# One weight fetch moved ahead of another in a decoder trunk, and the last quarter of its last row tile summed in a bank of its own

## The chip, the cores and the metric

The kernel runs on one core of a Trainium2 chip. The metric is the device time of one execution in microseconds (us), as the median of three runs. The engines are called as the profile calls them: PE (TensorE, the matmuls) with PEld (its weight loads), DVE (VectorE), ACT (ScalarE), POOL (GpSimd), and SP, whose queue issues the DMAs.

## What is computed

Two layers; each is a token mixer and then a convolutional feed-forward net, each followed by a residual sum and a LayerNorm. All is float32, for 256 tokens of 1024 channels.

```python
def mixer_sublayer(x, ...):
    proj = x @ w_in
    x_rnn, g_rnn, q_lat, kv_lat, k_rope, gate_a, gate_b = jnp.split(proj, _split_points(), axis=-1)
    y_rnn = jax.nn.gelu(g_rnn) * rg_lru(causal_dwconv(x_rnn, conv_w, conv_b), ...)
    y_mla = mla_attention(q_lat, kv_lat, k_rope, cos, sin, q_norm_g, w_uq, kv_norm_g, w_ukv)
    merged = jax.nn.sigmoid(gate_a) * y_rnn + jax.nn.sigmoid(gate_b) * y_mla
    return merged @ w_out

def conv_ffn(x, w_up, ffn_conv_w, ffn_conv_b, w_down):
    h = causal_dwconv(x @ w_up, ffn_conv_w, ffn_conv_b)
    h_gate, h_val = jnp.split(h, 2, axis=-1)
    return (jax.nn.gelu(h_gate) * h_val) @ w_down

for l in range(DEPTH):                                   # DEPTH = 2
    x = layer_norm(ALPHA * x + mixer_sublayer(x, ...), ln1_g[l], ln1_b[l])
    x = layer_norm(ALPHA * x + conv_ffn(x, ...), ln2_g[l], ln2_b[l])
```

Attention has 16 heads, is causal, and takes its values (64 per head) from `kv_lat` through a part of `w_ukv`. `gate_b` is 1024 columns wide.

## The kernel before

**Split products.** A float32 product is made of three matmuls on rounded parts: `mm3` (L193) multiplies high by high (L194), high by low (L195) and low by high (L196). So each weight block that arrives by DMA is split: ACT copies it into the high part (L185), DVE subtracts that from the raw block into the low part (L186). `load_split` (L169) issues the DMA on SP's queue and then both halves of the split. Raw blocks rotate through 4 buffers, split halves through 6 buffers named `w`; some weights go to slots named `wsh` and `wsl` instead.

**What sets the order.** PE runs in the order in which the program is written; the other engines' instructions are put in order when the program is built, by a scheduler that works on estimates of its own, and each engine then runs its list strictly in that order. Within a layer the mixer's steps are written in the order of the string `ORDER` (L43). A step is a letter and its arguments. Those that matter here:

- `P` with a hexadecimal digit fetches and splits one block of the list `FETCH` (L41) ahead of its use. `Pe` is the last, `("gb", 3)`: the weights of pair 3 (counted from 0) of branch B's gates. `h3` (`sig_b`, L672) multiplies them: 48 matmuls into the tile `proj`, then a sigmoid on ACT into `sB`.
- `w0` (`value_begin`, L734) fetches and splits the first half of the values' weights, one block of 128x1024; `v00` and `v01` (L738) use it, into `vps`.
- `b0`, `q0`, `k0`, `p0` and so on: for a group of four heads, fetch its query and key weights, multiply queries (`qps`), keys (`kps`) and rotary parts (`peps`), and copy them out of PSUM, half by ACT and half by DVE (for keys L731 and L732, into `k96`). `R1` and `r0`, `r1` are the recurrence's scan (L664) and its product with the gate (L668).
- `s`, `f`, `y`: scores of a pair of heads (`sps`; DVE L764 to L775, ACT L768 and L770), their transposes (`ptp`, which ACT copies to `pT`, L790), and the values (`yps`, L802). DVE multiplies `yps` by the sigmoid and adds branch A (`mg`, L809 and L810), and ACT and DVE split the sum into `mhi` (L199) and `mlo` (L200).
- `o01` and `o00` are the output projection of chunk 0 for row tiles 1 and 0; each tile has two of the four PSUM accumulators `oacc`.

**PSUM.** Two sets of four banks rotate: `acc` hands out the ones for `kps`, `qps`, `vps`, `oacc` and `dacc`, `bank` the ones for `proj`, `sps`, `ptp` and `yps`. A bank is free again when all who read its last tile have read it.

**The end of a layer.** `finish` (L360) issues the last products of the down projection for row tile 0, then LayerNorm's `tile` (L392) for it, then those of row tile 1 and its `tile`. A tile takes two halves of 512 columns: for each, residual plus sum (L400) and statistics (L404); then L405 and L406 on DVE, the inverse root on POOL (L407), and for the last layer L411 and L414 and the store.

Of the kernel before, what the change touches and what calls it, by code (L numbers as in the profile page):

```python
# [11 lines left out]
F32 = mybir.dt.float32  # L12
# [3 lines left out]
ALU = mybir.AluOpType  # L16

P = 128
# [24 lines left out]
ORDER = (  # L43
# [5 lines left out]
)  # L49
HELD = 4  # L50
WARM = 8
LINE = 256
STEP = 32
# [72 lines left out]
def trunk(ctx, tc, x_tok, x_chan, pos, wts, par, lnrow, consts, out):  # L126
    nc = tc.nc
    A = nc.scalar
    V = nc.vector
# [2 lines left out]

    cpool = ctx.enter_context(tc.tile_pool(name="cpool", bufs=1))
    tiny = ctx.enter_context(tc.tile_pool(name="tiny", bufs=2))
    wpool = ctx.enter_context(tc.tile_pool(name="wpool", bufs=1))
    big = ctx.enter_context(tc.tile_pool(name="big", bufs=1))
    sm = ctx.enter_context(tc.tile_pool(name="sm", bufs=2))
# [5 lines left out]
    def bank(name):  # L143
        return pp.tile([P, 512], F32, tag="pb", name=name)
# [48 lines left out]
    def mm3(o, lh, ll, rh, rl, start, stop):  # L193
        T.matmul(o, lhsT=lh, rhs=rh, start=start, stop=False)  # L194
        T.matmul(o, lhsT=lh, rhs=rl, start=False, stop=False)  # L195
        T.matmul(o, lhsT=ll, rhs=rh, start=False, stop=stop)  # L196
# [10 lines left out]
    spare = bank("spare")  # L207
    for _ in range(WARM):
        T.matmul(spare[:, :P], lhsT=idle, rhs=idle, start=True, stop=True)
# [23 lines left out]
    for i in range(1, 4):  # L233
# [9 lines left out]
        out=mask[:, P:], in_=mask[:, P:], pattern=[[-1, P]],  # L243
# [108 lines left out]
    def out_last(accs, t, n, wts_of, act_of, hc):  # L352
        for h, c in hc:
            hi, lo = wts_of(c)
            ah, al = act_of(c)
            mm3(accs[t][h], ah[:, t * P:(t + 1) * P], al[:, t * P:(t + 1) * P],
                hi[:, 512 * h:512 * h + 512], lo[:, 512 * h:512 * h + 512],
                False, c == n - 1)

    def finish(ln, accs, n, wts_of, act_of, late):  # L360
        out_last(accs, 0, n, wts_of, act_of, [(h, n - 1) for h in range(2)])
        ln.tile(0, accs)
        hc = [(h, c) for h in range(2) for c in range(n - late, n)]
        out_last(accs, 1, n, wts_of, act_of, hc[:-HELD])
        if not ln.last:
            ln.turn(0)
        out_last(accs, 1, n, wts_of, act_of, hc[-HELD:])
        ln.tile(1, accs)

# [8 lines left out]
    class LayerNorm:  # L378
# [10 lines left out]
            if not last:  # L389
                self.xs = [(slot("xhi", F32R), slot("xlo", F32R)) for _ in range(2)]  # L390

        def tile(self, t, accs):  # L392
            l, last = self.l, self.last
            z = big.tile([P, D], F32, tag="xres", name="z", bufs=4, align_bytes=LINE)
            st = tiny.tile([P, 2, 6], F32, tag="st", name="st")
            mv = tiny.tile([P, 2], F32, tag="mv", name="mv")
            rs = tiny.tile([P, 1], F32, tag="rs", name="rs")
            hs = [slice(512 * h, 512 * h + 512) for h in range(2)]
            for h in range(2):
                V.scalar_tensor_tensor(  # L400
                    out=z[:, hs[h]], in0=self.xres[t][:, hs[h]], scalar=ALPHA, in1=accs[t][h],
                    op0=ALU.mult, op1=ALU.add,
                )
                V.bn_stats(st[:, h], z[:, hs[h]])  # L404
            V.bn_aggr(mv, st.rearrange("p a b -> p (a b)"))  # L405
            V.tensor_scalar(out=rs, in0=mv[:, 1:2], scalar1=EPS, scalar2=None, op0=ALU.add)  # L406
            G.tensor_tensor(out=rs, in0=rs, in1=nhalf[:, 0:1], op=ALU.pow)  # L407
            g, b = self.gb
            if last:
                for h in range(2):  # L410
                    V.scalar_tensor_tensor(out=z[:, hs[h]], in0=z[:, hs[h]], scalar=mv[:, 0:1],  # L411
                                           in1=g[:, hs[h]], op0=ALU.subtract, op1=ALU.mult)
                for h in range(2):
                    V.scalar_tensor_tensor(out=z[:, hs[h]], in0=z[:, hs[h]], scalar=rs,  # L414
                                           in1=b[:, hs[h]], op0=ALU.mult, op1=ALU.add)
                    nc.sync.dma_start(out=out[t * P:(t + 1) * P, hs[h]], in_=z[:, hs[h]])
                return
            nmr = tiny.tile([P, 1], F32, tag="nmr", name="nmr")
            V.scalar_tensor_tensor(out=nmr, in0=mv[:, 0:1], scalar=-1.0, in1=rs,
                                   op0=ALU.mult, op1=ALU.mult)  # L420
            for c in (0, 256):
                V.tensor_scalar(out=z[:, c:c + 256], in0=z[:, c:c + 256], scalar1=mv[:, 0:1],
                                scalar2=rs, op0=ALU.subtract, op1=ALU.mult)
            A.activation(z[:, hs[1]], z[:, hs[1]], AF.Identity, scale=rs, bias=nmr)
            self.res.append(z)
# [84 lines left out]
    ends = (None, None)  # L510
    for l in range(DEPTH):
# [337 lines left out]
        later[0] = False  # L849
        ln = LayerNorm(l, 0, xres, False)  # L850
        finish(ln, oacc, 8, lambda c: ow[c], mer_of, 5)
        tp = [bank("upt") for _ in range(NB)]

# [85 lines left out]
        for j in range(NPAIR - LAG, NPAIR - 1):  # L939
            out_chunk(dacc, j, dw[j], hq[j], (0, 1) if j < NPAIR - LATE else (0,))  # L940
        ln = LayerNorm(l, 1, xres, l == DEPTH - 1)
        finish(ln, dacc, NPAIR, lambda c: dw[c], lambda c: hq[c], LATE)
        if l < DEPTH - 1:
            xs, xres = ln.xs, ln.res
            lat = []
            lacc = [[bank("latp") for _ in range(2)] for _ in range(NT)]
            for i, kc in enumerate(KORD):
                if i == 5:
                    ln.turn(1)
                    ends = ln.ends  # L950
# [113 lines left out]
```

## Time and profile before

| what | us |
|---|---|
| median of 3 runs (785.43 to 787.75) | 785.65 |
| the profiled execution, device time | 786.62 |
| its span, from the first to the last instruction | 784.8 |
| PE busy | 770.5 |
| DVE busy | 646.0 |
| ACT busy | 510.2 |
| PE idle for another engine, all waits of 0.2 us and more together | 6.5 |

The profiled execution is 0.97 us above the median, and 1.82 us of it lie outside the span. TensorE's granted clock is 0.995 of full speed over the span. A timeline row gives the start, the time to the end of the last instruction merged into the row, engine, line, operation, output and inputs, shape, and the count; the square brackets give the idle time ahead of it and who ended that. DVE and ACT rows overlap a little, since an instruction starts before the one ahead has drained. PE's matmuls overlap by more than half, so for PE it is the distance of starts that counts.

### The profile page before, as it was taken

What the parts mean: (1) busy time and instruction counts of PE and PEld (TensorE: products, weight loads), DVE (VectorE), ACT (ScalarE), POOL (GpSimd) and SP (SyncE); (2) the same over time, 40 slices, a digit from 0 to 9 for tenths busy, and PEclk for the clock granted to TensorE, in tenths of its full rate; (3) what the DMA queues carried; (4) which work ended last, traced back from release to release, by engine and by line L of the source; (5) the groups of instructions that cost most, each with busy time, mean ns of one, the idle gap of its engine ahead of it and who ended that gap; (6) DMA issues with size and microseconds to landing.
All of it is one profiled execution on the core that took longest, in us unless ns stands there. A gap on an engine that the chain in (4) does not pass through costs nothing.

```text
span 784.8 us, 14452 instructions
## 1 busy us (share of the span) xinstructions
PE 770.5 (98%) x5712; PEld 723.9 (92%) x5712; DVE 646.0 (82%) x1260; ACT 510.2 (65%) x910; POOL 10.2 (1%) x27
## 2 busy tenths in 40 slices
PE   9999899999999999999999999999999999999996
PEld 9999899878999999999899999998799999999994
DVE  6998789997699977668777897999877998677665
ACT  6856887783677565556374579688657775565540
POOL 0000000000000000000000000000000000000000
PEclk9999999999999999999999999999999999999999
DMA  9855436525457555535715554463515675746311
GB/s 320 331 210 215 151 112 240 207 63 210 162 199 262 203 199 210 195 126 196 268 52 218 169 208 134 172 231 123 193 76 186 261 251 182 247 162 200 123 54 54
DMA packets 26467, 144.76 MB, mean 184 GB/s; under 512 B 3360, under 2 KB 7072, under 8 KB 11808
## 3 DMA queue, kind: packets, MB, share of 16 engines
q1 hardware_dynamic: 26400, 143.84, 51.7%
q8 instruction: 45, 0.74, 0.4%
q14 instruction: 22, 0.18, 0.1%
HBM read 140.68 MB, written 1.05 MB: 181 GB/s over the span
## 4 chain that ended last, share of the span: by engine, by line
PE 89%; DVE 4%; ACT 4%; issue 2%; DMA 1%; SPq 0%; DVEq 0%
PE proj L196 16%; PE proj L194 15%; PE proj L195 15%; PE dacc L194 6%; PE dacc L195 6%; PE dacc L196 6%; PE oacc L194 2%; PE oacc L196 2%; PE oacc L195 2%; PE sps L759 2%; DVE w L186 2%; PE yps L802 2%; PE ptp L787 1%; PE latp L195 1%; PE latp L196 1%
## 5 line engine op out<-in xcount | busy, mean ns | idle before, releaser
L196 PE MATMUL proj<-xhi,w 128*128 128x256 f32 x1216 | 338.0, 278 | 3.0 <-DVE w L186 3.0
L194 PE MATMUL proj<-xhi,w 128*128 128x256 f32 x1216 | 338.1, 278 | 0.0
L195 PE MATMUL proj<-xlo,w 128*128 128x256 f32 x1216 | 337.7, 278 | 0.0
L186 DVE TENSOR_TENSOR w<-raw,w 128x1024 fp32r<-128x1024 f32 (+5 forms) x226 | 241.8, 1087 | 52.4 <-ACT w L185 51.9
L185 ACT ACTIVATE w<-raw 128x1024 fp32r<-128x1024 f32 (+5 forms) x226 | 208.8, 952 | 86.6 <-PE proj L196 73.4
L196 PEld LDWEIGHTS proj<-xhi,w 128*128 128x128 f32 x1216 | 228.8, 188 | 3.4 <-DVE w L186 3.4
L195 PEld LDWEIGHTS proj<-xlo,w 128*128 128x128 f32 x1216 | 229.2, 189 | 1.3
L194 PEld LDWEIGHTS proj<-xhi,w 128*128 128x128 f32 x1216 | 228.9, 188 | 1.4
L905 DVE SCALAR_TENSOR_TENSOR u<-proj,par,u 128x255 f32<-128x255 f32 (+1 forms) x176 | 83.4, 478 | 25.4 <-ACT u L902 23.3
L902 ACT ACTIVATE u<-proj,par 128x256 f32<-128x256 f32 x88 | 49.7, 564 | 72.7 <-DVE u L905 47.8
L194 PE MATMUL dacc<-wsh,hh 128*128 128x512 f32 x192 | 75.2, 392 | 0.0
L195 PE MATMUL dacc<-wsl,hh 128*128 128x512 f32 x192 | 75.1, 391 | 0.0
L196 PE MATMUL dacc<-wsh,hl 128*128 128x512 f32 x192 | 74.7, 389 | 0.0
L186 DVE TENSOR_TENSOR wsl<-raw,wsh 128x1024 fp32r<-128x1024 f32 (+2 forms) x66 | 70.4, 1077 | 0.0
L185 ACT ACTIVATE wsh<-raw 128x1024 fp32r<-128x1024 f32 (+2 forms) x66 | 59.5, 938 | 0.0
L196 PEld LDWEIGHTS dacc<-wsh,hl 128*128 128x128 f32 x192 | 36.1, 188 | 7.8
L194 PEld LDWEIGHTS dacc<-wsh,hh 128*128 128x128 f32 x192 | 36.0, 188 | 6.4
L195 PEld LDWEIGHTS dacc<-wsl,hh 128*128 128x128 f32 x192 | 36.1, 188 | 6.0
L199 ACT ACTIVATE hh<-u 128x256 fp32r<-128x256 f32 x48 | 19.8, 411 | 24.7 <-DVE u L913 24.6
L194 PE MATMUL oacc<-w,mhi 128*128 128x512 f32 x64 | 26.7, 417 | 0.0
L196 PE MATMUL oacc<-w,mlo 128*128 128x512 f32 x64 | 25.3, 395 | 0.0
L195 PE MATMUL oacc<-w,mhi 128*128 128x512 f32 x64 | 25.2, 393 | 0.0
(213 smaller groups left out, 1130.2 us busy)
## 6 DMA issues: line engine op xcount, KB each, us to landing
raw<-in_wts SPq DMA_DIRECT2D x114, 1024.0 KB, 4.9
raw<-in_wts SPq DMA_DIRECT2D x8, 832.0 KB, 4.9
gb<-in_lnrow SPq DMA_DIRECT2D x8, 512.0 KB, 7.7
raw<-in_wts SPq DMA_DIRECT2D x4, 672.0 KB, 4.0
raw<-in_wts SPq DMA_DIRECT2D x7, 336.0 KB, 6.1
raw<-in_wts SPq DMA_DIRECT2D x4, 512.0 KB, 4.8
xres<-in_x_tok SPq DMA_DIRECT2D x2, 512.0 KB, 6.0
k<-krot SPq DMA_DIRECT2D x8, 128.0 KB, 2.4
```

Source lines behind the costliest of these rows:

```text
L185: behind(A.activation(h, w, AF.Copy), after[0])
L186: lo_ins = V.tensor_tensor(out=lo[:, c - a:d - a], in0=w, in1=h.bitcast(F32), op=ALU.subtract)
L194: T.matmul(o, lhsT=lh, rhs=rh, start=start, stop=False)
L195: T.matmul(o, lhsT=lh, rhs=rl, start=False, stop=False)
L196: T.matmul(o, lhsT=ll, rhs=rh, start=False, stop=stop)
L199: A.activation(hi, src, AF.Copy)
L759: T.matmul(sps[:, P:P + S], lhsT=q96[:, h4, P:], rhs=k96[:, h4], start=True, stop=True)
L787: T.transpose(ptp[:, b * P:(b + 1) * P], sns[hh][:, b * P:(b + 1) * P], ident)
L802: T.matmul(yps[hh * 64:hh * 64 + 64, t * P:S], lhsT=vs[:, hv:hv + 64], rhs=pts[hh][:, 2 * t * P:(2 + t) * P], start=t == 0, stop=t == 1)
L902: ea = A.activation(dst, src, AF.Identity, scale=pcol(l, "fw", 96 + ch), bias=pcol(l, "fb", ch))
L905: ev = V.scalar_tensor_tensor(out=dst[:, k:], in0=src[:, :S - k], scalar=pcol(l, "fw", 48 * (2 - k) + ch), in1=dst[:, k:], op0=ALU.mult, o ...
```

## The change

There are two edits. The first is in `ORDER`: `Pe` moves from behind `p0` to the place of `w0`, ahead of `R1`, and `w0` moves behind `h3`. The scheduler then orders all engines but PE anew. The second is in `finish` and `tile`, for the last layer's second LayerNorm alone. The last `ENDS` (3) chunks of row tile 1's second half, nine matmuls of 512 columns, become eighteen of 256: first nine into columns 512 to 767 of the old accumulator, then nine into a bank of their own, `dend`, for columns 768 to 1023. DVE adds `dend` to the last quarter behind the statistics of the third. A tile of 48 floats, `gap`, moves later buffers by 256 bytes.

```diff
-    "e3 a2 Pc N a3 h1 R0 Pd h2 h0 b0+ w0 R1 p0 Pe h3 q0 b1+ r0 L1+ b2 k0 v01 p1 r1 s0 q1 "
+    "e3 a2 Pc N a3 h1 R0 Pd h2 h0 b0+ Pe R1 p0 h3 w0 q0 b1+ r0 L1+ b2 k0 v01 p1 r1 s0 q1 "
 HELD = 4
+ENDS = 3
...
+    tiny.tile([P, 48], F32, name="gap", bufs=1)
...
+    def out_split(accs, t, n, wts_of, act_of, late):
+        ends = bank("dend")[:, :256]
+        for dst, a in ((accs[t][1][:, :256], 512), (ends, 768)):
+            for c in range(n - late, n):
+                hi, lo = (w[:, a:a + 256] for w in wts_of(c))
+                ah, al = (x[:, t * P:(t + 1) * P] for x in act_of(c))
+                mm3(dst, ah, al, hi, lo, a == 768 and c == n - late, c == n - 1)
+        return ends
...
         hc = [(h, c) for h in range(2) for c in range(n - late, n)]
+        if ln.last:
+            out_last(accs, 1, n, wts_of, act_of, hc[:-ENDS])
+            ln.tile(1, accs, out_split(accs, 1, n, wts_of, act_of, ENDS))
+            return
         out_last(accs, 1, n, wts_of, act_of, hc[:-HELD])
-        if not ln.last:
-            ln.turn(0)
+        ln.turn(0)
...
-        def tile(self, t, accs):
+        def tile(self, t, accs, ends=None):
...
-            st = tiny.tile([P, 2, 6], F32, tag="st", name="st")
+            st = tiny.tile([P, 3, 6], F32, tag="st", name="st")
...
+            cuts = hs if ends is None else [hs[0], slice(512, 768), slice(768, 1024)]
             for h in range(2):
                 V.scalar_tensor_tensor(
                     out=z[:, hs[h]], in0=self.xres[t][:, hs[h]], scalar=ALPHA, in1=accs[t][h],
                     op0=ALU.mult, op1=ALU.add,
                 )
-                V.bn_stats(st[:, h], z[:, hs[h]])
-            V.bn_aggr(mv, st.rearrange("p a b -> p (a b)"))
+                V.bn_stats(st[:, h], z[:, cuts[h]])
+            if ends is not None:
+                V.tensor_tensor(out=z[:, cuts[2]], in0=z[:, cuts[2]], in1=ends, op=ALU.add)
+                V.bn_stats(st[:, 2], z[:, cuts[2]])
+            V.bn_aggr(mv, st[:, :len(cuts)].rearrange("p a b -> p (a b)"))
```

DVE's list around `h3` in layer 0, before (`w_1473` is the values' block, `w_1502` and `w_1505` are the halves of pair 3's weights, the others are query and key weights):

```order
L664 SCALAR_TENSOR_TENSOR th_1233<-ga_336,gx_334 128x1024
L186 TENSOR_TENSOR w_1465<-raw0_1460,w_1465 128x896
L186 TENSOR_TENSOR w_1473<-raw0_1471,w_1473 128x1024
L186 TENSOR_TENSOR w_1502<-raw0_1500,w_1502 128x1024
L186 TENSOR_TENSOR w_1505<-raw0_1500,w_1505 128x1024
L186 TENSOR_TENSOR w_1581<-raw0_1579,w_1581 128x768
```

The same place after (lines are 2 higher there ahead of `finish`, and 20 behind `tile`; `w_1474` and `w_1477` are pair 3's, `w_1555` is the values'):

```order
L188 TENSOR_TENSOR w_1466<-raw0_1461,w_1466 128x896
L188 TENSOR_TENSOR w_1474<-raw0_1472,w_1474 128x1024
L188 TENSOR_TENSOR w_1477<-raw0_1472,w_1477 128x1024
L188 TENSOR_TENSOR w_1582<-raw0_1580,w_1582 128x768
L484 STREAM_SHUFFLE pet_1493<-pet_1493 128x256
L485 TENSOR_TENSOR pet_1493<-pet_1493,cosT_175 128x256
L486 TENSOR_TENSOR pet_1493<-pet_1493,sinT_176 128x256
L487 TENSOR_TENSOR pet_1493<-pet_1493 128x256
L188 TENSOR_TENSOR w_1555<-raw0_1553,w_1555 128x1024
```

The values' split has moved from ahead of pair 3's to five rows behind them; from there to the next `k96` copy the list holds the same instructions as before.

DVE's list where the keys of the last group of heads leave PSUM (the copy into `k96`), before:

```order
L809 TENSOR_TENSOR mg_2094<-yps_2089,sB_1346 128x256
L732 COPY k96_1869<-kps_2074 64x2x256
L772 RECIPROCAL rsum_2037<-rsum_2037 128x2
L810 TENSOR_TENSOR mg_2094<-mg_2094,th_1226 128x256
L186 TENSOR_TENSOR w_2101<-raw0_2099,w_2101 128x512
L773 TENSOR_SCALAR sn_2053<-sn_2053,rsum_2037 128x128
L775 TENSOR_SCALAR sn_2053<-sn_2053,rsum_2037 128x256
L186 TENSOR_TENSOR w_2101<-raw0_2099,w_2101 128x512
```

And after:

```order
L829 TENSOR_TENSOR mg_2095<-yps_2090,sB_1347 128x256
L792 RECIPROCAL rsum_2038<-rsum_2038 128x2
L830 TENSOR_TENSOR mg_2095<-mg_2095,th_1227 128x256
L188 TENSOR_TENSOR w_2102<-raw0_2100,w_2102 128x512
L793 TENSOR_SCALAR sn_2054<-sn_2054,rsum_2038 128x128
L795 TENSOR_SCALAR sn_2054<-sn_2054,rsum_2038 128x256
L188 TENSOR_TENSOR w_2102<-raw0_2100,w_2102 128x512
L752 COPY k96_1870<-kps_2075 64x2x256
```

The copy has moved behind six instructions.

ACT's list where it copies the transposes of head pair 5 (`pT`), before:

```order
L770 ACTIVATE sn_2167,rsum_2151<-sn_2167,nm_2168 128x256
L790 ACTIVATE pT_2237<-ptp_2233 128x384
L768 ACTIVATE sn_2212,rsum_2208<-sn_2212,nm_2213 128x128
L790 ACTIVATE pT_2243<-ptp_2239 128x384
L770 ACTIVATE sn_2212,rsum_2208<-sn_2212,nm_2213 128x256
L199 ACTIVATE mhi_2181<-mg_2183 128x256
```

And after:

```order
L790 ACTIVATE sn_2168,rsum_2152<-sn_2168,nm_2169 128x256
L201 ACTIVATE mhi_2182<-mg_2184 128x256
L187 ACTIVATE wsh_2191<-raw0_2189 128x512 x2
L788 ACTIVATE sn_2213,rsum_2209<-sn_2213,nm_2214 128x128
L790 ACTIVATE sn_2213,rsum_2209<-sn_2213,nm_2214 128x256
L187 ACTIVATE wsh_2197<-raw0_2189 128x512 x2
L810 ACTIVATE pT_2238<-ptp_2234 128x384
L810 ACTIVATE pT_2244<-ptp_2240 128x384
```

Seven instructions now stand ahead of the first copy, of which one stood between the copies and two behind them, and four are weight splits (`wsh`) that came later. Layer 1 has the same three moves.

## Rows read from the trace of the kernel before

**Rows 1.** Page, part 1: busy time, share of the span, instructions of each engine.

```profile
PE 770.5 (98%) x5712; PEld 723.9 (92%) x5712; DVE 646.0 (82%) x1260; ACT 510.2 (65%) x910; POOL 10.2 (1%) x27
```

**Rows 2.** PE's waits: engine, line, waited for: us in total, times, longest.

```profile
PE proj L196 <- DVE w L186: 3.0, 2, 1.5
```

**Rows 3.** Timeline of PE, start of `h3` in layer 0.

```profile
115.05 0.28 PE L194 MATMUL proj<-xhi,w 128*128 128x256 f32 x1
115.16 0.28 PE L195 MATMUL proj<-xlo,w 128*128 128x256 f32 x1
116.95 0.38 PE L196 MATMUL proj<-xhi,w 128*128 128x256 f32 x1 [1.51 <-DVE w L186]
```

**Rows 4.** Timeline of DVE, from ahead of `h3` to the first key copy.

```profile
113.56 5.34 DVE L186 TENSOR_TENSOR w<-raw,w 128x896 fp32r<-128x896 f32 x5
...
123.83 2.58 DVE L186 TENSOR_TENSOR w<-raw,w 128x512 fp32r<-128x512 f32 x4 [0.19 <-ACT w L185]
...
127.92 0.69 DVE L732 COPY k<-kps 64x512 f32<-64x512 f32 x1
```

**Rows 5.** Timeline of PE, scores of the first pair's second head.

```profile
129.02 0.38 PE L757 MATMUL sps<-k,q 96*128 96x128 f32 x2
```

**Rows 6.** Timeline of DVE, from the last key copy to pair 4's merge.

```profile
160.34 0.69 DVE L732 COPY k<-kps 64x512 f32<-64x512 f32 x1
160.95 0.15 DVE L772 RECIPROCAL rsum<-rsum 128x2 f32<-128x2 f32 x1
...
162.41 1.88 DVE L186 TENSOR_TENSOR w<-raw,w 128x512 fp32r<-128x512 f32 x3
...
166.97 0.41 DVE L809 TENSOR_TENSOR mg<-yps,sB 128x256 f32<-128x256 f32 x1
...
167.99 0.42 DVE L810 TENSOR_TENSOR mg<-mg,th 128x256 f32<-128x256 f32 x1
```

**Rows 7.** Timeline of PE, first matmul into the last key copy's bank.

```profile
162.17 0.39 PE L194 MATMUL oacc<-w,mhi 128*128 128x512 f32 x1
```

**Rows 8.** Timeline of ACT around the copies of pair 5's transposes.

```profile
163.13 0.42 ACT L199 ACTIVATE mhi<-mg 128x256 fp32r<-128x256 f32 x1
163.44 1.15 ACT L185 ACTIVATE w<-raw 128x512 fp32r<-128x512 f32 x2
...
165.60 0.39 ACT L768 ACTIVATE sn<-sn,nm 128x128 f32<-128x128 f32 x1
...
165.99 0.50 ACT L770 ACTIVATE sn<-sn,nm 128x256 f32<-128x256 f32 x1
...
168.47 0.49 ACT L790 ACTIVATE pT<-ptp 128x384 f32<-128x384 f32 x1 [1.89 <-PE ptp L787]
...
169.24 0.48 ACT L790 ACTIVATE pT<-ptp 128x384 f32<-128x384 f32 x1
```

**Rows 9.** Timeline of PE, values of pair 5.

```profile
170.01 0.87 PE L802 MATMUL yps<-pT,v 128*64 128x256 f32 x8
```

**Rows 10.** Timeline of PE, the last matmul.

```profile
776.76 0.39 PE L196 MATMUL dacc<-wsh,hl 128*128 128x512 f32 x1
```

**Rows 11.** Timeline of DVE at the end.

```profile
775.86 0.69 DVE L404 BATCH_NORM_STATS2 st<-z 128x6 f32<-128x512 f32 x1
777.18 0.69 DVE L400 SCALAR_TENSOR_TENSOR z<-z,dacc 128x512 f32<-128x512 f32 x1 [0.64 <-PE dacc L196]
777.90 0.69 DVE L404 BATCH_NORM_STATS2 st<-z 128x6 f32<-128x512 f32 x1
778.63 0.21 DVE L405 BATCH_NORM_AGGREGATE mv<-st 128x2 f32<-128x12 f32 x1
```

**Rows 12.** Groups by line and shape: busy us, mean ns of one, idle before.

```profile
L200 DVE TENSOR_TENSOR mlo<-mg,mhi 128x256 fp32r<-128x256 f32 x16 | 6.7, 419 | 1.5 <-ACT mhi L199 1.0
```

**Rows 13.** The same view of PE's and PEld's largest groups.

```profile
L194 PE MATMUL proj<-xhi,w 128*128 128x256 f32 x1216 | 338.1, 278 | 0.0
L194 PEld LDWEIGHTS proj<-xhi,w 128*128 128x128 f32 x1216 | 228.9, 188 | 1.4
```

## The prediction

> **What bounds the kernel now.** I read the page's busy times first, then PE's waits, then the timelines of PE, DVE and ACT around each place where the change moves something. PE is busy for 770.5 us of 784.8 [rows 1], so time can only be won where PE stands idle. Its longest wait for another engine is at `h3`: 3.0 us in two waits, one per layer [rows 2]. In layer 0 the first two matmuls of `h3` start at 115.05 and 115.16, and the third, the first that needs a low half, starts at 116.95 after 1.51 us of idle time [rows 3]. What it waits for is DVE: from 113.56 DVE runs five weight splits without a gap [rows 4], and by the order list the second is the values' block, which nobody needs yet, ahead of the first half of pair 3's weights. The other idle time that the change can reach is the end: PE's last matmul ends at 777.15 [rows 10], 7.65 us before the span does.
>
> The reader should also see what is not in the list of waits. Through the attention PE waits for nobody, but with little to spare. The first key copy on DVE ends at 128.61 [rows 4] and the scores that read it start at 129.02 [rows 5]: 0.41 us. The last key copy ends at 161.03 [rows 6] and the first matmul into its bank starts at 162.17 [rows 7]: 1.14 us. The first copy of pair 5's transposes on ACT ends at 168.96 [rows 8] and its reader starts at 170.01 [rows 9]: 1.05 us; the second ends at 169.72 and is read some 0.3 us later than the first.
>
> **Part 1, the fetch.** The DMA count, the split count and PE's work stay the same; only places in queues change. On SP's queue the pair's block is now issued one place earlier and the values' block one place later, both long before they are split, so I take 0 for the transfers. The price if that cover were gone would be one wait for a block; no row of PE's waits shows one.
>
> *At `h3`.* Five splits of 4736 columns together take 5.34 us [rows 4], so one of 1024 takes 1.15. That one leaves the front: the low half comes 1.15 us earlier, and 0.36 of the wait stays. Gain on PE: 1.15 us per layer.
>
> *At the first key copy.* DVE has no slack here. From 113.56 to the copy its only named idle time is 0.19 us, for ACT [rows 4], and the list up to the copy holds the same instructions as before. So PE comes 1.15 earlier and the copy at most some 0.3 (the 0.19, and about 0.1 where a start slips behind ACT). PE then arrives at 127.87 and needs a copy that ends at 128.3 to 128.4, with about 0.05 us for the signal: a new wait of 0.4 to 0.6; I take 0.45. The margin of 0.41 is spent, and 0.70 of the gain is left.
>
> *At the last key copy.* It now stands behind six more instructions: in the trace these run from 160.95 to the end of the first of the three splits at 162.41, that is to 163.0 [rows 6], 2.06 us. If DVE is as much earlier as PE here, both shift alike and the wait is 2.06 less the margin of 1.14, 0.92. Small gaps on DVE that close may give 0.25 back (0.65); if DVE does not come earlier with PE, since it is full, it may be 0.92 + 0.70 = 1.6. I take 0.85, near the first, since DVE's row starts from `yps`, which PE delivers earlier. PE is now 0.15 later than before. `kps` shares its bank with `oacc`, and that is why PE is the one who waits.
>
> *At pair 5's transposes.* ACT stood idle for 1.89 us ahead of the first copy [rows 8], but now has in front of it the split of pair 4's merge and six more instructions. The merge (L810) stood at 167.99, behind two score instructions [rows 6]; now it follows L809 directly. L809 at 166.97, or up to 0.8 earlier, gives a merge that ends at 167.0 to 167.85. Then ACT: `mhi` 0.31 from start to start (163.13 to 163.44), two splits 1.05, two exponentials 0.88 (0.39 and 0.50), two splits 1.05 [rows 8], 3.3 in all, and the first copy 0.49. It ends at 170.8 to 171.65, while PE wants it at 170.01 + 0.15. The wait is 0.65 to 1.5, with 0.1 more for the second copy. I take 0.82 for both, near the low end, since DVE's list is shorter by then by what the key copy let past.
>
> Per layer that is -1.15 + 0.45 + 0.85 + 0.82 = +0.97, and for two layers +1.94. All lows give +0.5 per layer; 1.6 at the last key copy gives +1.7.
>
> **Part 2, the end.** PE's work stays: nine matmuls of 512 columns become eighteen of 256. Matmuls of 256 columns start 0.11 us apart (115.05 and 115.16 [rows 3]), half the distance of 512, also where each loads weights of its own, for 0.188 us [rows 13], under the others.
>
> [...] I take 0 for PE.
>
> On DVE the sum of the half (L400) no longer waits for the last matmul but for the ninth of eighteen, ending 1.02 earlier, at 776.13. It still starts only at 776.47, since the statistics of the first half run from 775.86 [rows 11] and the next instruction follows 0.61 behind, as behind the copy of 512 columns [rows 6]. So: sum 776.47 to 777.16; statistics of 256 columns from 777.19, for 0.42 (a shape that this trace lacks; other operations take 0.69 for 512 columns, as the statistics do [rows 11], and 0.419 for 256 [rows 12]), start to start 0.34; the added sum of 256 from PSUM 777.53 to 777.95; statistics again to 778.40; aggregate at 778.43, against 778.63 [rows 11]. Gain 0.20. If the quarter's statistics and sum cost as much as those for a half, 0.69, the aggregate starts at 779.2 and the end loses 0.6; if the statistics' fixed part is small, it gains 0.35. I take 0.20, since L200's row is the nearest.
>
> **Sum.** +1.94 - 0.20 = +1.74 on a profiled execution of 786.62 (span 784.8), so a span of 786.5. On the median of 785.65, which lies 0.97 below that execution, it gives **787.4 us**, 0.22% more. A measurement of this kernel tells a change from none at about 0.3%, or 2.36 us: under 783.3 is faster, over 788.0 is slower.
>
> **The rivals.**
>
> *DVE does not come earlier (slower).* One mechanism, at the last key copy: DVE is full, so the moved copy costs PE 1.5 to 1.6. Per layer -1.15 + 0.45 + 1.55 + 0.82 = +1.67, in all +3.1: 788.8. For it: DVE's row from 160.34 to 166.97 has hardly a gap [rows 6]. Against it: L809 reads what PE delivers, so the row starts earlier with PE. It crosses 788.0 from 1.15 us at that place on, the others as taken. 0.25.
>
> *The change doesn't do what it says (slower).* If pair 3's weights are no sooner there, because the ACT half waits for a free `w` buffer, the 1.15 is not gained while the copy (0.92) and the transposes (0.7) still cost: +3.0, 788.7. Against it: ACT's half of the first split was ready when PE began at 115.05 [rows 3]. 0.03.
>
> *The moved copies find idle time.* Only the first key copy costs: -0.70 per layer, and -0.20: 784.05, within 0.3%. For it: ACT's 1.89 us of idle time [rows 8]. Against it: PE's margins are smaller than what was put in front. 0.11.
>
> *The full gain.* -1.15 per layer with no new wait, and 0.35 at the end: -2.65, 783.0, faster. For it: PE waits nowhere in the attention today. Against it: the 0.41 at the first key copy, where the list of DVE is unchanged. 0.04.
>
> *The weight loads lie open at the end.* Nine loads of 0.188, 1.7 us, on top of the forecast: 789.1, slower. [...] 0.02.
>
> **How the numbers follow.** The forecast, new waits at all three places (786.2 to 788.0), has 0.55. Slower by over 0.3%: 0.25 + 0.03 + 0.02 = 0.30. Faster: 0.04. Within: 0.55 + 0.11 = 0.66. The range leaves out the two gains (0.15 together) and reaches over the slower cases short of their ends: 785.2 to 789.0.
>
> **What the profile after would show.** PE's wait at `h3` falls to about 0.4 us per layer. If I am right, three lines are new in PE's waits, each twice: `sps` for DVE's key copy (0.3 to 0.6), `oacc` for the same copy (0.65 to 1.6), `yps` for ACT's `pT` (0.6 to 1.5). The statistics of a quarter take about 0.42, and the aggregate starts some 1.3 us after PE's last matmul ends, not 1.48. I am wrong if PE's list of waits in the attention stays empty, or if `h3` still waits for over 1 us.

## The result, and the profile after

The changed kernel takes 790.87 us (median of 5 runs, 790.06 to 792.59) against 785.94 for the kernel before on the same chip (5 runs): the ratio is 1.0062, with a 95% interval of 1.0047 to 1.0076, so 3.7 to 6.0 us more. The prediction of record was 787.4 us, in a range of 785.2 to 789.0. The profiled execution has a span of 789.0 us, 4.2 more than before.

The page's first part after the change, to be read against [rows 1]: PE is busy for 2.1 us more, although it does the same products with nine more instructions.

```profile
PE 772.6 (98%) x5721; PEld 724.6 (92%) x5721; DVE 646.9 (82%) x1262; ACT 510.9 (65%) x910; POOL 10.9 (1%) x27
```

PE's waits after (engine, line, waited for: us in total, times, longest), against [rows 2]:

```profile
...
PE oacc L196 <- DVE k L752: 1.7, 2, 0.9
PE yps L822 <- ACT pT L810: 1.3, 2, 0.7
...
PE latp L196 <- ACT w L187: 1.0, 1, 1.0
PE sps L777 <- PE sps L779: 0.9, 2, 0.6
PE proj L198 <- DVE w L188: 0.8, 2, 0.4
...
```

The wait at `h3` fell from 3.0 to 0.8 us, and three new ones came, each in both layers, at the three places that the prediction named. The next four fences show layer 0.

`h3` on PE (start, time, line, shape, idle time ahead and who ended it), against [rows 3]. The third matmul starts 0.66 us behind the second, 1.13 less than before:

```profile
114.38 0.28 PE L197 MATMUL proj<-xlo,w 128*128 128x256 f32 x1
115.04 0.39 PE L198 MATMUL proj<-xhi,w 128*128 128x256 f32 x1 [0.38 <-DVE w L188]
```

The first key copy on DVE, then the scores on PE, against [rows 4, 5]. The view names PE as the releaser; the row of DVE says who it was: the copy ends at 127.47, the scores start at 127.57.

```profile
126.78 0.69 DVE L752 COPY k<-kps 64x512 f32<-64x512 f32 x1
...
127.57 0.46 PE L777 MATMUL sps<-k,q 96*128 96x128 f32 x2 [0.55 <-PE sps L779]
```

The last key copy on DVE, now behind a weight split, and the first matmul into its bank, against [rows 6, 7]. DVE's row there begins with a product that reads `yps`, at 159.89 before (first fence) and at 158.59 after:

```profile
159.89 0.41 DVE L809 TENSOR_TENSOR mg<-yps,sB 128x256 f32<-128x256 f32 x1
```

```profile
158.59 0.42 DVE L829 TENSOR_TENSOR mg<-yps,sB 128x256 f32<-128x256 f32 x1
...
160.44 0.68 DVE L188 TENSOR_TENSOR w<-raw,w 128x512 fp32r<-128x512 f32 x1
161.16 0.69 DVE L752 COPY k<-kps 64x512 f32<-64x512 f32 x1
...
160.65 0.40 PE L198 MATMUL oacc<-w,mlo 128*128 128x512 f32 x1
161.91 0.50 PE L196 MATMUL oacc<-w,mhi 128*128 128x512 f32 x1 [0.86 <-DVE k L752]
```

Pair 5's copies on ACT, behind the four `wsh` splits, and their reader, against [rows 8, 9]:

```profile
167.12 1.14 ACT L187 ACTIVATE wsh<-raw 128x512 fp32r<-128x512 f32 x2
...
169.04 1.14 ACT L187 ACTIVATE wsh<-raw 128x512 fp32r<-128x512 f32 x2
170.08 0.84 ACT L810 ACTIVATE pT<-ptp 128x384 f32<-128x384 f32 x2
...
169.56 0.39 PE L198 MATMUL oacc<-w,mlo 128*128 128x512 f32 x1
170.60 0.80 PE L822 MATMUL yps<-pT,v 128*64 128x256 f32 x3 [0.66 <-ACT pT L810]
```

**Where the 4.2 us are.** PE issues the same matmuls in the same order up to the last nine, so the start of each can be subtracted from its start before. This difference moves at a few places:

| place | after minus before, us |
|---|---|
| first latent weights (start of the program) | +0.70 |
| 83 to 89 us | -1.48 |
| layer 0: `h3` / `sps` / `oacc` / `yps` / rest of the mixer | -1.37 / +0.75 / +1.16 / +1.07 / +0.10 |
| feed-forward net of layer 0 | +0.54 |
| start of layer 1 | -0.53 |
| layer 1: `h3` / `sps` / `oacc` and `yps` / rest | -0.91 / +0.60 / +2.24 / +0.03 |
| feed-forward net of layer 1 | +1.54 |
| the end, to the aggregate of the last tile | -0.22 |

The sum is 4.22. The first two lines belong to these two executions, not to the change: the wait for the first latent weights differs from execution to execution, 0.3 us before, 1.0 after, up to 1.8 (e4 below), and from 83 to 89 us the execution before ran with a granted clock of 0.72 in the mean, the one after with 1.00. In both, PE had stood idle at the gates for 1.44 or 1.45 us; before, the granted clock was then 0.50 from 84.5 to 87.9 us, and after it stayed at 1.00 (columns: us, PE busy and instructions, granted clock, DMA share, GB/s; the first row is of before, the second of after):

```profile
83.00:89.00 6.00, 4.56 (x26) 0.72 0.65 242
```

```profile
83.00:89.00 6.00, 4.35 (x36) 1.00 0.61 228
```

With the new ORDER and the old end (e1 below) the granted clock also differed between executions of one kernel: 0.996 in the mean of the profiled one, 0.998 or 0.999 in the other four. Without the two lines the change costs 5.0 us, as the medians say (4.93). Of that, 3.7 us are in the two mixers, -0.2 at the end, and 1.5 us in places of which the prediction says nothing: the matmuls of the feed-forward nets and of layer 1's start.

**Two paces.** A block of the up projection is 48 matmuls of 256 columns into `proj`, followed by `dacc`; PE waits for nobody in them. These are the first row of three blocks in a row of layer 1 and the first row behind each, before:

```profile
639.38 0.28 PE L194 MATMUL proj<-xhi,w 128*128 128x256 f32 x1
...
644.89 0.40 PE L194 MATMUL dacc<-wsh,hh 128*128 128x512 f32 x1
...
647.63 0.28 PE L194 MATMUL proj<-xhi,w 128*128 128x256 f32 x1
...
653.18 0.40 PE L194 MATMUL dacc<-wsh,hh 128*128 128x512 f32 x1
...
655.93 0.28 PE L194 MATMUL proj<-xhi,w 128*128 128x256 f32 x1
...
661.44 0.40 PE L194 MATMUL dacc<-wsh,hh 128*128 128x512 f32 x1
```

and three blocks after:

```profile
642.65 0.28 PE L196 MATMUL proj<-xhi,w 128*128 128x256 f32 x1
...
648.30 0.40 PE L196 MATMUL dacc<-wsh,hh 128*128 128x512 f32 x1
...
651.03 0.28 PE L196 MATMUL proj<-xhi,w 128*128 128x256 f32 x1
...
656.69 0.40 PE L196 MATMUL dacc<-wsh,hh 128*128 128x512 f32 x1
...
659.43 0.28 PE L196 MATMUL proj<-xhi,w 128*128 128x256 f32 x1
...
664.94 0.40 PE L196 MATMUL dacc<-wsh,hh 128*128 128x512 f32 x1
```

Before, the blocks last 5.51, 5.55 and 5.51 us; after, 5.65, 5.65 and 5.51, and this repeats every three blocks to the end of the layer. Inside a block the starts are 113 or 114 ns apart, or 117 to 119. A block of 5.65 has the slow pace throughout, one of 5.51 for some 15 matmuls and one of 5.55 for 24; then it turns fast and stays so. Counted over all neighbours in `proj` (3596), 1227 are slow before (116 to 123 ns) and 1604 after. A block's weights lie in two of the six slots of `w`, and three pairs of slots take turns. The slots start 8320 bytes apart, so in the built program they start alternately 192 bytes (call it A) and 64 bytes (B) beyond a multiple of 256. The pairs before and after, with the time of their blocks:

| | layer 0 | layer 1 |
|---|---|---|
| before | A-B 5.51, B-B 5.65, A-A 5.65 | A-B 5.51, B-A 5.55, A-B 5.51 |
| after | B-B 5.65, B-A 5.55, A-A 5.65 | A-A 5.65, B-B 5.65, A-B 5.51 |

(Only the last but one block of layer 0 is out of turn, with A-A in both kernels.) In the feed-forward nets the time goes with the pair in every block: a block turns fast behind its first step from an A slot to a B slot, and one that has no such step stays slow. The new ORDER gave the blocks other slots. The product `upt`, which goes ahead of them, fits: its weights lie in `wsh` and `wsl`, at multiples of 256 bytes alone, and 186 of its 188 distances are 116 to 121 ns, both before and after.

### The profile page after: what moved, and what is told of

Its sections match the earlier page's. It is cut to its first block, busy times and chain, and to the rows that moved or that the text cites. A ratio compares the mean times of both kernels' runs of the same rounds, so it can differ in the third digit from the quotient of the medians.

```text
span 789.0 us, 14463 instructions
## 1 busy us (share of the span) xinstructions
PE 772.6 (98%) x5721; PEld 724.6 (92%) x5721; DVE 646.9 (82%) x1262; ACT 510.9 (65%) x910; POOL 10.9 (1%) x27
```

## The experiments

**The two edits apart (e1, e2).** e1 is the ORDER line of the change alone, e2 the end and `gap` alone.

> The ORDER edit alone, with the old end. In the changed kernel PE's matmuls of 256 columns into proj run at two paces, about 113 and 118 ns from start to start, and 391 more of them than before run at the slow one, nearly all in the two feed-forward nets. Theory (buffers): the new order gives the blocks of the feed-forward nets other slots of w, and a pair of slots sets the pace; the ORDER edit then brings both the waits (sps, oacc, yps on DVE and ACT: +2.2 us net) and the slow paces (about 1.8 us more): 790 to 791.5 us against 785.9, with some 1600 slow matmuls. Rival (end): the slow paces come from the 256 bytes by which gap moves the later buffers, or from the end; then this kernel has the waits alone, some 1200 slow matmuls and 788 to 788.6 us.

> The edit at the end and gap alone, with the old ORDER. Theory (buffers): the pairs of slots are those of before, so the paces stay (about 1200 slow matmuls into proj), PE's list of waits is that of before, and the end is about 0.2 us shorter: 785.5 to 786.0 us. Rival (end): the shift of 256 bytes makes the paces slow: about 1600 slow matmuls and 787.4 to 788 us.

e1 measured 791.1 us against 786.9, ratio 1.0059 (1.0047 to 1.0071): the ORDER edit alone costs what the whole change costs. e2 measured a ratio of 1.000 (0.9989 to 1.001), no change that can be told; its gain of 0.2 is below that. Both expectations reckon from 785.9; the kernel before, measured beside them, had 786.9, so e2's 787.04 lies above its range. (The counts of slow matmuls in these expectations stop at 121 ns, so they are a little lower than above.) e1 has 1616 slow matmuls and e2 1270. The blocks are the clearest: the 36 blocks of the two nets last 202.08 us in e1 as in the changed kernel, and 200.25 in e2 as before. So `gap` and the end have no part in the paces. e1's waits:

```profile
PE oacc L194 <- DVE k L732: 1.7, 2, 0.9
PE yps L802 <- ACT pT L790: 1.3, 2, 0.7
...
PE sps L757 <- PE sps L759: 1.0, 2, 0.6
PE proj L196 <- DVE w L186: 0.8, 2, 0.4
```

**The paces alone (e3, e4, e9).** In all three the ORDER and the end are those of before; only the place of the low halves or of the slots moves. In e3 the low half of a block starts 128 bytes further:

```diff
-                hi, lo = both[:, :1024], both[:, 1024:2048]
+                hi, lo = both[:, :1024], both[:, 1024 + STEP:]
```

> The kernel before, with the low half of each block in w placed 128 bytes further, in the padding that is there already, so that high and low halves of one block lie at addresses that differ by an odd multiple of 128 bytes. Theory (buffers): a stream of matmuls leaves the slow pace where the weights' address steps from an odd to an even multiple of 128 bytes; that is now once in every three matmuls, so fewer than 150 matmuls into proj are slow in place of 1204, about 1060 times 4.5 ns: -4.8 us, 780.5 to 782 us. Rival (contention): the pace follows what DVE, ACT or the DMA queues do at that time and not an address: no change, 785.5 to 786.5 us.

e4 has `STEP = 0` in place of 32 (floats), so that all six slots are A slots (buffers behind them move by 768 bytes, a multiple of 256):

> The kernel before without the 128 bytes of padding in each slot of w, so that all slots have the same parity of 128 bytes. Theory (buffers): no step from odd to even is left, nearly all 3648 matmuls into proj run at 118 ns, 2450 more than before at 4.5 ns each: +11 us, 796 to 798 us. Rival (contention): the padding changes nothing: 785.5 to 786.5 us.

e9 moves the low halves by 64 bytes (`both[:, 1040:2064]`):

> The kernel before, with the low halves moved by 64 bytes in place of the 128 of e3. It asks what distance counts. Theory (parity of 128 bytes): 64 bytes leave both halves of a slot in lines of the same parity at their start, so the paces stay near those of before, 1000 to 1300 slow matmuls and 785.5 to 787 us. Rival (any odd distance): what counts is that the addresses of the two halves differ by anything but a multiple of 256 bytes; then fewer than 200 are slow and the time is 781 to 782 us.

The row of before is that of e3 and e4; beside e9 it measured 787.36.

| kernel | us | ratio to before (95%) | slow matmuls | 36 blocks, us |
|---|---|---|---|---|
| before | 786.9 | | 1227 | 200.25 |
| e3, low halves +128 bytes | 781.47 | 0.9931 (0.9920 to 0.9943) | 137 | 196.25 |
| e4, all slots A | 792.55 | 1.0071 (1.0058 to 1.0083) | 2874 | 203.44 |
| e9, low halves +64 bytes | 796.43 | 1.0119 (1.0103 to 1.0136) | 2857 | 203.75 |

One block of layer 1 in e3 (5.45 us):

```profile
635.25 0.28 PE L194 MATMUL proj<-xhi,w 128*128 128x256 f32 x1
...
640.70 0.40 PE L194 MATMUL dacc<-wsh,hh 128*128 128x512 f32 x1
```

e3 and e4 refute the rival that the paces come from what DVE, ACT or the DMA queues do: in the built programs every engine's list is that of before, instruction for instruction, and the addresses alone move the time by 5.4 us down and 5.6 up. In e3 PE's wait at `h3` is 3.0 us as before, and PE is busy for 765.7 of 779.6 us, the same 98%. e3 gains what its 1090 fewer slow matmuls are worth (4.9 at 4.5 ns, and some in `qps` and `kps`). e4 came out below its expectation of 796 to 798: some 620 matmuls in the first part of layer 1, from about 425 us to the wait at `h3` at 503 us, are fast there although all slots are A, so an A-to-B step is not the only thing that turns a stream fast. At 4.5 ns each that is 2.8 us; the wait at `h3` is also 0.9 us shorter (2.1 in place of 3.0), and the rest of the miss was not traced. e9 fell outside both theories: neither "nothing changes" nor "fast", but the slowest of all, with starts from 113 to 124 ns mixed within a block. So the theory of A and B tells the time of every block of the feed-forward nets whose halves lie a multiple of 128 bytes apart, and nothing about 64.

**The waits alone (e5).** The changed kernel with e3's line:

> The changed kernel with the low halves moved by 128 bytes, as in e3. Theory (waits and paces are two costs that add up): the 1604 slow matmuls go (fewer than 200 left, -6.3 us), the waits at sps, oacc and yps stay as they are in the changed kernel; against e3 (781.5 us) the +2.2 of the waits and the -0.2 of the end remain: 783.2 to 784.2 us. Rival (one cost): the waits come from the slow paces and go with them; then 781 to 781.5 us, and PE's list of waits loses oacc and yps.

It measured 785.16 us against 786.98, ratio 0.9979 (0.9968 to 0.9989), with 177 slow matmuls. Its waits are those of the changed kernel:

```profile
PE oacc L196 <- DVE k L752: 1.8, 2, 0.9
PE yps L822 <- ACT pT L810: 1.3, 2, 0.7
PE sps L777 <- PE sps L779: 1.1, 2, 0.5
...
PE proj L198 <- DVE w L188: 0.8, 2, 0.4
```

The rival falls: the waits don't go with the paces. But the theory's number was too low as well: against e3 it is 3.7 us, not 2.0. PE's starts in e5 less those in e3, both at the fast pace: `h3` -1.11 and -1.14, `sps` +0.73 and +0.84, `oacc` with `yps` +2.25 and +2.30, in all +3.9, and -0.2 at the end. The idle times of the lists make only 2.0: 4.2 us of new waits less 2.2 at `h3`. A wait costs more than its idle time: at `oacc` in the changed kernel the list says 0.86, but the start is 1.26 us behind the one ahead where 0.23 is the rule (1.03 more), and the next distance is 0.34 in place of 0.23. PE's rows overlap, so the idle time counts from the modelled end of the last matmul, and the overlap is lost too (0.17: the row takes 0.40, and 0.23 is the distance). At `yps` the list has the wait for the first copy alone (0.66). The first matmul starts 0.73 us later against those ahead of it, and the second, which reads the second copy, another 0.26; that wait lies under the modelled end of the first.

**Where the places in the queues come from (e6, e7, e8).** All three have e3's line. e6 has the new ORDER and writes `U1+` later:

```diff
-    "L2+ f4 o01 L3 o00 s6 y4 U1+ o21 s7 f5 o11 y5 o10 f6 o40 o20 f7 y6 o30 y7 o50 o60 U0+"
+    "L2+ f4 o01 L3 o00 s6 y4 o21 s7 f5 U1+ o11 y5 o10 f6 o40 o20 f7 y6 o30 y7 o50 o60 U0+"
```

> e3 with the changed ORDER and one step more moved: U1+, which fetches and splits the up projection's second block into wsh and wsl, is written behind f5, the step with pair 5's copies into pT, in place of ahead of o21. Theory (queue places): ACT then copies pT ahead of the four wsh splits, so the waits at yps (1.3 us) go and those at oacc (1.7 us) stay: some 1.6 us below the changed ORDER with the old U1+, 782 to 782.6 us. Rival (late DVE): pT is late because the merge is late on DVE; then yps waits as before and the time is 783.5 to 784 us.

It measured 783.35 us, ratio 0.9957 (0.9943 to 0.9971), 1.8 us below e5 in the same comparison, and 2.0 with the 0.2 that e5's new end gains and e6 lacks. The time lies above the expected range, since the changed ORDER that it starts from costs more than was expected (e5). The list decides: `yps` is gone from it, the rest stays:

```profile
PE oacc L194 <- DVE k L732: 1.8, 2, 0.9
...
PE sps L757 <- PE sps L759: 0.8, 2, 0.5
PE proj L196 <- DVE w L186: 0.8, 2, 0.4
```

PE's starts fall by 1.10 us in each layer at `yps`: that is its price, where the list said 0.65. In layer 0 the merge (`mg`) starts at 167.18 in e6 and at 167.05 in e5, so it came no earlier, but the first copy into `pT` starts at 169.35 in place of 170.79. The `wsh` splits ahead of the copies were the cause, not a late merge.

e7 is the order of before with `Pe` and `w0` next to each other:

```diff
-    "e3 a2 Pc N a3 h1 R0 Pd h2 h0 b0+ w0 R1 p0 Pe h3 q0 b1+ r0 L1+ b2 k0 v01 p1 r1 s0 q1 "
+    "e3 a2 Pc N a3 h1 R0 Pd h2 h0 b0+ Pe w0 R1 p0 h3 q0 b1+ r0 L1+ b2 k0 v01 p1 r1 s0 q1 "
```

> e3 with Pe at the place of w0 and w0 directly behind it, ahead of R1 (the change has it behind h3). Theory (queue places): DVE splits pair 3 ahead of the values, as in the changed kernel, and the later lists of DVE and ACT are those of before; the wait at h3 falls to 0.8 us, the wait of sps for the first key copy comes (0.9 us), those at oacc and yps do not: 1.2 us below e3, 780.0 to 780.6 us. Rival (any earlier fetch upsets the lists): oacc and yps wait as after the change, 783 to 784 us.

It measured 780.93 us, ratio 0.9928 (0.9909 to 0.9947). PE's list has 0.8 us at `sps`, and neither `oacc` nor `yps` is in it, so an earlier fetch of pair 3 need not upset the attention; it was the values' fetch behind `h3` that did. PE's starts against e3 are 0.38 lower in layer 0 (-1.15 at `h3`, +0.77 at `sps`) and 0.32 in layer 1, 0.7 in all where 1.2 was expected. In the times this can't be told from e3's 0.9931: two thirds of layer 0's gain at `h3` go into the key copy. In layer 1, `h3`'s matmuls run mostly at 117 to 124 ns, in e6 and e8 too, and take 0.23 us more than in e5, where the same kind of pair (A-A, low halves apart) is fast. So e3's line doesn't make every stream fast.

e8 adds the changed end to e7 and writes `k0` ahead of `b1+`; PE's order stays (the edit is against the changed kernel):

```diff
-    "e3 a2 Pc N a3 h1 R0 Pd h2 h0 b0+ Pe R1 p0 h3 w0 q0 b1+ r0 L1+ b2 k0 v01 p1 r1 s0 q1 "
+    "e3 a2 Pc N a3 h1 R0 Pd h2 h0 b0+ Pe w0 R1 p0 h3 q0 k0 b1+ r0 L1+ b2 v01 p1 r1 s0 q1 "
```

> The changed end, the low halves apart as in e3, the order of e7, and k0 written ahead of b1+ (PE's order stays; only DVE and ACT copy the first keys ahead of the splits that b1+ and L1+ bring). Theory (queue places): the wait at sps goes too, so that the whole 1.15 us per layer at h3 is kept, -2.3 us, and -0.2 at the end: 778.6 to 779.4 us against e3's 781.5. Rival (DVE is full): the splits that now stand behind the copy are late for the next users, and PE waits for w there instead: 779.8 to 781 us.

It measured 778.16 us, ratio 0.9892 (0.9874 to 0.9909): by the ratio 8.5 us below the kernel before, and the lowest of both kernels and of all that were tried. It is also below the expected range. Part of that is not the kernel's: three of its four executions had a granted clock of 0.998, and 14 of the 17 of before 0.997 or less (of before, those at 0.998 took 784.76 to 786.06 us, those at 0.996 or less 786.86 to 788.95). PE's starts against e3 fall by 1.15 us in layer 0 and 0.82 in layer 1 at `h3`, which with the end's 0.2 makes 2.2 us, inside the expectation. DVE now copies the first keys ahead of a weight split,

```profile
124.88 0.69 DVE L752 COPY k<-kps 64x512 f32<-64x512 f32 x1
125.48 0.95 DVE L188 TENSOR_TENSOR w<-raw,w 128x768 fp32r<-128x768 f32 x1
```

and in PE's list of waits (the last one left out is 0.2 us at the gates) nothing is left of `sps`, `oacc` and `yps`:

```profile
PE gates L197 <- DVE xcl L631: 2.0, 2, 1.4
PE spare L211 <- DVE lruw L339: 1.1, 1, 1.1
PE proj L198 <- DVE w L188: 0.8, 2, 0.4
PE latp L196 <- ACT w L187: 0.3, 1, 0.3
...
```

## Why the prediction was wrong

The sign and the three places were right; the sizes of the new waits were not, and one mechanism was missing. Step by step:

- **`h3`: right.** Forecast -1.15 per layer. The third matmul's start moves by -1.13 against the second's in both layers of e5 and e7 against e3; by the end of the multiplication it is -1.11 and -1.14 in e5, and -1.15 in layer 0 of e7, while in its layer 1 the slower pace takes some 0.3 back.
- **The first key copy: right in its mechanism.** DVE's copy came 0.36 earlier (forecast "at most some 0.3") where PE came 1.13 earlier, so PE waits for the copy. The margin was 0.41, the new wait 0.71 in layer 0 against the 0.45 taken: 0.24 of the difference is PE's own, since the matmuls of `h3` ran at the fast pace after and at the slow one before. The net of `h3` and the copy is -0.62 in layer 0, forecast -0.70.
- **The last key copy: right place, the term too small.** Relative to PE the copy starts 2.12 us later (forecast 2.06) and the margin was 1.14, so the first reasoning gave 0.92 and the start moved by 1.03. I took 0.85, below the 0.92, for small gaps that would close; none did. With the slower restart it is 1.16. The rival "DVE does not come earlier" is refuted: DVE's row came 1.30 us earlier (158.59 against 159.89), and so did PE.
- **Pair 5's transposes: right place, the term too small.** Forecast 0.65 to 1.5, taken 0.82 "near the low end"; 1.07 to 1.10 in the runs. The first copy's wait was near what was taken (0.73), but the second's, put at 0.1, was 0.26, and the slower restart was left out.
- Together the three new waits were taken as 2.12 us per layer and cost 3.0 (e5 against e3: +2.98 and +3.14): 1.6 to 1.9 us of the miss (the first by the table above). The first key copy came out above its bounds (0.73 and 0.84 in e5 against 0.4 to 0.6), the other two inside theirs, and all three had been taken below the middle. The sum let only the last key copy go to its upper bound, so even its worst case (+1.7 per layer) lies under what came (+1.9 and +2.0).
- **The sentence that failed** is the first of part 1: PE's work stays the same and "only places in queues change". With it goes the premise ahead of it, that "time can only be won where PE stands idle": e3 won 5.4 us with PE's waits as they were. A fetch that moves also takes another slot, and all fetches behind it. The slots set the pace of the matmuls that read them: +1.83 us in the 36 blocks, +1.5 net with layer 1's start. That is about the other half of the miss of 3.2 us. No term, no rival and no bound held this, though the blocks of before, 5.51 to 5.65 us long in turn, had both paces in them. The chance of 0.30 for slower by over 0.3% went to three other mechanisms, and the runs show none of them.
- **The end: right.** Forecast 0.20; from PE's rows 0.22. The statistics of a quarter take 0.43 (0.42 forecast), and the chain runs from the half's sum to the aggregate as written, against [rows 11]:

```profile
780.90 0.67 DVE L417 SCALAR_TENSOR_TENSOR z<-z,dacc 128x512 f32<-128x512 f32 x1
781.61 0.43 DVE L421 BATCH_NORM_STATS2 st<-z 128x6 f32<-128x256 f32 x1
781.95 0.40 DVE L423 TENSOR_TENSOR z<-z,dend 128x256 f32<-128x256 f32 x1
782.39 0.43 DVE L424 BATCH_NORM_STATS2 st<-z 128x6 f32<-128x256 f32 x1
782.85 0.24 DVE L425 BATCH_NORM_AGGREGATE mv<-st 128x2 f32<-128x18 f32 x1
```

- **The weight loads at the end lie under the matmuls.** The last eighteen start 0.12 us apart (the last two at 781.29 and 781.41), each with a load of its own of 0.19 us, and take 0.1 more than nine of 512 columns took. No run shows the 1.7 us of the rival in which nine loads of 0.188 us lie open.

What stays open is why an A-to-B step turns a stream fast, why some streams are fast without one (e4) or slow in spite of it (`h3` in layer 1 of e6 to e8), and why 64 bytes make all of it slow: the runs show that the place of the weights changes the pace, not through what part of the chip. In e3, e4 and e9 the weights' addresses alone move the distance of two matmuls, from 113 or 114 ns in e3 to 117 to 119 in e4 and 113 to 124 in e9.

## What to carry to other kernels

Where a scheduler and a pool stand between the text and the chip, a step that moves changes three things: the queues, the order that the scheduler makes of them, and the buffers that all later blocks get; compare the buffers' addresses of the two builds too. Take the distance of starts of one kind of matmul stage by stage: if the same block has two durations with no wait in it, look at where its operands lie before anything else is tuned. And price a new wait on PE by the start that is displaced and by the restart, not by the idle time that the list shows: here 1.15 us for a listed 0.86, and 1.1 for a listed 0.65, where a second wait doesn't show in the list.

## What the runs showed of the hardware that was not expected

In these kernels matmuls of 256 columns with a weight load each run at 113 or at 118 ns from start to start, in the feed-forward nets by where the weights lie: low halves that start 128 bytes off the high halves' residue (modulo 256) give 5.45 us for 48 of them, equal residues 5.65 where no other slot comes in, and 64 bytes off 5.65 to 5.69. The pace has a memory: before, a stream that had turned fast stayed so for 275 distances in a row (34.7 to 65.9 us) and for 228 (88.1 to 113.9), while the first 11 to 47 distances of each block behind `dacc` were slow, 11 behind the transposes `ltT` of layer 0 and 44 behind layer 0's wait at `h3`; the 44 behind layer 1's wait were fast, and e4's first part of layer 1 stayed fast for some 77 us with no step at all. A kernel with the same instructions thus takes from 781.5 to 796.4 us by the place of the low halves alone.
